# Four planning passes over the main region, ordered first layers of the experts, and scattered expert rows, in a one-core fp32 block kernel

## The chip, the cores and the metric

The kernel runs on one core of one Trainium2 chip. The core has TensorE (PE in the rows: matmuls and transposes; PEld is its weight load), VectorE (DVE), ScalarE (ACT), GpSimd (POOL), SyncE (SP, which here only issues transfers) and 16 DMA engines. The metric is the time of one execution in microseconds of device time. A profiled execution also leaves a trace with the start and end of each instruction, what released it, and the clock granted to TensorE.

## What is computed

512 tokens of width 1024, batch 1, all in fp32. Cut to what matters:

```python
# first block
mod = silu(c) @ ada_w + ada_b                      # 1024 x 3072
shift, scale, gate = split(mod, 3)
h = rmsnorm(x, norm_g) * (1 + scale) + shift
p = h @ w_in
y = concat(rwkv7(p[..., :RWKV_COLS]), stick_breaking(p[..., RWKV_COLS:])) @ w_out
x = rmsnorm(x + gate * y, final_g)
# second block
x = layernorm(a * x + gated_delta_net(x))          # 8 q/k heads, 16 v heads, two directions
for grp in range(4):                               # 32 experts, top 1 of 4 groups, then top 2 of its 8
    h = silu(x @ w_gate[grp]) * (x @ w_up[grp])
    out += (h * comb[grp]) @ w_down[grp]
x = layernorm(a * x + out)
x = x + sigmoid(x @ pe_w_gate) * (p_2 @ pe_w_proj)
```

## The kernel before, in words

**A planner stands behind all code.** `Kern` (phase1, phase2, phase3) never issues an instruction itself. Each call, such as `V.tensor_tensor(...)`, is recorded by `Rec` as an operation with its engine, tiles, cost in a model, and successors. `Rec.run` then lays the tiles out in SBUF and PSUM and emits the operations region by region in the order that `Rec.order` returns. So all instructions have one source line, that of `emit` (L738), and the names of SBUF in the trace are those of memory zones: S_0_87, S_0_90, S_0_94 are arenas that hold many tiles, P_0_135 is PSUM. `order` (L554) is a list scheduler: it walks a model of the five queues forwards, and among the operations of an engine that are ready it takes the one with the highest `rank`, which is the longest chain of costs from the operation to the end (`cp`), plus a bonus per stage (`AHEAD`), plus a little noise. Each engine carries out its own list strictly in that order. `MIX` seeds the random order in which tiles get their places in memory. There are three regions: region 0 is everything up to an If around nine overflow blocks, region 1 is those blocks (skipped with these inputs), region 2 is the end of the kernel. `nc.edge(a, b)` lets the operations b start only after the operations a.

**High and low halves.** A matmul of fp32 values is made of three (`mm3`, L811): each operand is split into a rounded part hi (cast by ACT) and a rest lo (subtraction on DVE, `split`, L794), and hi by hi, hi by lo and lo by hi are added up in PSUM. So each piece of weights costs an ACT cast and a DVE subtraction.

**Setup (phase1, L838).** The four token chunks of x are loaded, scaled and transposed into `xnT` (8 tiles of 128 features by 512 tokens). `mod` has 24 columns of 128: each is a dot product of a 128 x 1024 piece of `ada_w` with c, on DVE (`scalar_tensor_tensor` with `accum_out`). For each of the 8 tiles k two columns (scale 8+k, shift k) are needed before h is formed by a DVE `tensor_scalar` and split into `hTh` and `hTl`, on which the matmuls with `w_in` wait. The columns 16 to 23 are the gate, used only behind `out1`, far later; their loads and dot products stand in the code behind the 8 tiles of h.

**Middle.** RWKV and stick breaking are generators whose steps are interleaved by `STEPS` (L762, L1260), then `out1`, then the gated delta net: heads, `prep`, and for four groups (gq) of heads `invert` (L1508), which inverts 32x32 triangles on DVE in a chain of 60 dependent steps of shrinking width (`inv32`, L1313) between DVE transposes, then `scan` and `finish`. Then layer norm and the routing (L1827 on), where a one-hot matmul `ptab` gives for each of 16 blocks of 112 slots (NP = 16, NS = 112, NB = 25) the token `gidx` that a slot holds.

**Experts (L2039 `block`).** Block b serves two experts, s = 0 and 1. POOL gathers its 112 rows (`xe`, indirect DMA from x_d), PE transposes them (112x112), and for each s: the first layer `pgu` (24 matmuls of 128x512, gate and up at once), silu on ACT, product with the mask on DVE (`hs`), two transposes of `hs`, a split into `hT`; then the second layer `pd` (12 matmuls per s). Weights come by SP into a ring of 22 pieces `raw` of 512 KB, 12 pieces per block. The result `ys` is copied by ACT and written by SP to rows b*112 and on of `y_d`. Blocks 16 to 24 of `y_d` are filled with zeros by SP, with 9 writes from the middle of the kernel.

**End (L2110 on).** POOL gathers for each chunk of 128 tokens and each of its two experts the rows of `y_d` by `yidx` (8 indirect DMAs of 128 x 1024), DVE adds them with their weights, then layer norm, transposes, the matmuls of the output gate, and the result.

## Time and profile before

| | |
|---|---|
| three runs | 1583.02, 1584.03 (median), 1599.12 us |
| the profiled execution | 1593.17 us; its span (first to last instruction) 1591.3 us |
| PE busy | 1436.6 us (90%), PEld 1189.3 us (75%) |
| DVE, ACT, POOL busy | 1151.9 us (72%), 963.3 us (61%), 193.8 us (12%) |
| transfers | 273.40 MB, mean 172 GB/s |
| mean granted TensorE clock | 0.953 |

Busy times say how long an engine was at work, not whether it was waited for. Since PE is busy for 90% of the span, what matters is where the other 10% lies and what ended each of its waits. So the table by stage comes first, and then the waits inside a stage.

### The profile page before, as it was taken

What the parts mean: (1) busy time and instruction counts of PE and PEld (TensorE: products, weight loads), DVE (VectorE), ACT (ScalarE), POOL (GpSimd) and SP (SyncE); (2) the same over time, 40 slices, a digit from 0 to 9 for tenths busy, and PEclk for the clock granted to TensorE, in tenths of its full rate; (3) what the DMA queues carried; (4) which work ended last, traced back from release to release, by engine and by line L of the source; (5) the groups of instructions that cost most, each with busy time, mean ns of one, the idle gap of its engine ahead of it and who ended that gap; (6) DMA issues with size and microseconds to landing.
All of it is one profiled execution on the core that took longest, in us unless ns stands there. A gap on an engine that the chain in (4) does not pass through costs nothing. (4 is left out here: it accounts for less than half of the span.)

```text
span 1591.3 us, 25168 instructions
## 1 busy us (share of the span) xinstructions
PE 1436.6 (90%) x8865; PEld 1189.3 (75%) x8865; DVE 1151.9 (72%) x2281; ACT 963.3 (61%) x2029; POOL 193.8 (12%) x334
## 2 busy tenths in 40 slices
PE   5989999999989885999999999999958999999948
PEld 3677777777978764887988788988847777777736
DVE  7995348865565589898995797553567888888863
ACT  4426455555246876579677856663447777777821
POOL 2101111112010222012101300000120000000040
PEclk7999999799999897999999999999969999999969
DMA  9321111214333754234523641575268999999442
GB/s 379 120 80 54 41 49 58 97 41 132 107 119 113 220 192 146 69 118 156 164 99 129 199 136 58 195 283 209 91 224 276 348 361 355 346 362 354 149 163 80
DMA packets 118023, 273.40 MB, mean 172 GB/s; under 512 B 12416, under 2 KB 53632, under 8 KB 116864
## 3 DMA queue, kind: packets, MB, share of 16 engines
q1 hardware_dynamic: 114688, 263.31, 47.5%
q0 software_dynamic: 3200, 8.39, 1.6%
q8 instruction: 72, 1.18, 0.3%
q14 instruction: 63, 0.52, 0.1%
HBM read 231.81 MB, written 42.99 MB: 173 GB/s over the span
## 5 line engine op out<-in xcount | busy, mean ns | idle before, releaser
L738 PE MATMUL P<-S 128*128 128x512 f32 (+6 forms) x4659 | 942.7, 340 | 91.2 <-DVE S L738 50.6
L738 PEld LDWEIGHTS P<-S 128*128 128x128 f32 (+3 forms) x4659 | 676.5, 181 | 231.2 <-DVE S L738 65.6
L738 PE MATMUL P<-S,S 128*128 128x512 f32 (+12 forms) x4206 | 765.7, 315 | 57.1 <-DVE S L738 43.0
L738 PEld LDWEIGHTS P<-S,S 128*128 128x128 f32 (+4 forms) x4206 | 560.1, 178 | 163.9 <-DVE S L738 35.1
L738 DVE TENSOR_TENSOR S<-S,S 128x512 fp32r<-128x512 f32 (+17 forms) x607 | 474.4, 804 | 171.4 <-ACT S L738 136.2
L738 ACT CAST S<-S 128x512 fp32r<-128x512 f32 (+2 forms) x457 | 365.7, 821 | 293.8 <-PE P L738 238.5
L738 ACT ACTIVATE S<-S 128x128 f32<-128x128 f32 (+7 forms) x433 | 209.2, 517 | 89.8 <-DVE S L738 59.6
L738 DVE SCALAR_TENSOR_TENSOR S<-S 128x512 f32<-128x512 f32 (+3 forms) x302 | 182.6, 632 | 46.2 <-ACT S L738 36.1
L738 DVE TENSOR_TENSOR S<-S 128x256 f32<-128x256 f32 (+32 forms) x414 | 148.5, 372 | 9.2 <-ACT S L738 3.0
L738 ACT COPY S<-P 128x512 f32<-128x512 f32 (+5 forms) x224 | 109.1, 497 | 70.7 <-PE P L738 65.0
L738 ACT ACTIVATE S<-P,S 128x128 f32<-128x128 f32 (+1 forms) x325 | 110.5, 411 | 58.3 <-PE P L738 48.7
L738 ACT ACTIVATE S<-P 128x512 f32<-128x512 f32 (+6 forms) x226 | 87.0, 401 | 54.0 <-PE P L738 49.7
L738 POOL TENSOR_SCALAR_AFFINE_SELECT S<-S 128x128 f32<-128x128 f32 (+2 forms) x137 | 62.0, 466 | 325.7 <-DVE S L738 118.0
L738 DVE TENSOR_TENSOR S<-P,S 128x512 f32<-128x512 f32 (+4 forms) x131 | 75.2, 586 | 31.8 <-ACT S L738 26.1
L738 POOL MEMSET S<- 128x2 f32 (+9 forms) x102 | 27.0, 275 | 365.8 <-DVE S L738 353.4
L738 DVE SCALAR_TENSOR_TENSOR S<-P,S,S 128x128 f32<-128x128 f32 (+2 forms) x165 | 58.4, 366 | 15.7 <-PE P L738 14.3
L738 DVE SCALAR_TENSOR_TENSOR S<-S,S 128x128 f32<-128x128 f32 (+5 forms) x121 | 54.8, 485 | 12.3 <-POOL S L738 7.8
L738 DVE SCALAR_TENSOR_TENSOR S<-S,P 128x128 f32<-128x128 f32 (+2 forms) x112 | 45.0, 429 | 24.7 <-PE P L738 20.1
L738 POOL TENSOR_TENSOR S<-S,S 128x8 f32<-128x8 f32 (+2 forms) x22 | 35.2, 1601 | 219.3 <-DVE S L738 218.5
L738 ACT CAST S<-P 128x224 fp32r<-128x224 f32 (+2 forms) x80 | 36.0, 477 | 39.4 <-PE P L738 38.2
L732 ACT ACT_TABLE_LOAD x45 | 57.7, 1283 | 0.8
L738 POOL DMA_INDIRECT S<-x_d,S x16 | 25.4, 1588 | 255.7 <-PE P L738 237.9
(34 smaller groups left out, 318.7 us busy)
## 6 DMA issues: line engine op xcount, KB each, us to landing
S<-in_moe_w_dram SPq DMA_DIRECT2D x192, 512.0 KB, 6.9
S<-in_gw_in_dram SPq DMA_DIRECT2D x48, 512.0 KB, 4.4
S<-in_w_in_dram SPq DMA_DIRECT2D x29, 512.0 KB, 3.5
S<-in_ada_dram SPq DMA_DIRECT2D x24, 512.0 KB, 8.5
y_d<-S SPq DMA_DIRECT2D x25, 448.0 KB, 6.5
gdn<-S SPq DMA_DIRECT2D x40, 256.0 KB, 3.1
S<-gdn SPq DMA_DIRECT2D x8, 1280.0 KB
S<-gcT_d SPq DMA_DIRECT2D x64, 128.0 KB, 3.3
```

The costliest lines, as they stand in the source:

```text
L732: self.nc.scalar.preload_act_table_set(o.load)
L738: return getattr(self.real[o.eng], o.method)(*[real(x) for x in o.args], **{n: real(x) for n, x in o.kw.items()})
```

## The change

Six edits, in one diff:

1. `Rec.plan` schedules region 0 up to four times (`PASSES`). After each pass `back` walks the finished schedule backwards with the same model of the queues and writes into `tail` how long before the end each operation has to start; the next pass ranks by `tail` in place of `cp`. The pass whose model ends earliest is kept. `MIX` goes from 18 to 13, which places tiles elsewhere.
2. The eight gate columns with their loads move into a group "mod" behind the fourth of the interleaved RWKV and stick-breaking steps.
3. h is formed by ACT (`activation`, Identity, with scale and bias columns) in place of a DVE `tensor_scalar`.
4. `y_d` has one row per token and expert choice (2 x 512 rows). A block writes its rows with an indirect DMA on POOL to the rows in `sidx` (slots without a token are dropped), the end reads 8 plain pieces by SP, and the zero writes are gone. For this `ptab` has 76 columns in place of 50.
5. `gu_last`: the first matmul of each first layer `pgu` waits for the last matmul of the first layer before it, over s and over blocks.
6. `yidx` is gone, `sidx` is computed by one more DVE operation and two ACT operations.

```diff
-    MIX = 18
+    MIX = 13
+    PASSES = 4
+    def back(self, ids):
...
+                    heapq.heappush(q, (-ops[i].start - 1e9 * ops[i].held, i))
...
+            o.tail = end
...
+    def plan(self, ids, t0):
...
+        for k in range(self.PASSES):
...
+            got = self.order(ids, t0, k)
+            end = max(ops[i].end for i in ids)
+            if best is None or end < best[0]:
...
-            o.rank = o.cp + self.AHEAD.get(o.group, 0.0) + 1e9 * o.held
+            o.rank = (o.tail if k else o.cp) + self.AHEAD.get(o.group, 0.0) + 1e9 * o.held
...
-                    for i in self.order(ids, self.t_end):
+                    for i in (self.order if n else self.plan)(ids, self.t_end):
...
-            V.tensor_scalar(xnT[:, k], xnT[:, k], mod[:, 8 + k:9 + k], mod[:, k:k + 1], ALU.mult, ALU.add)
+            A.activation(xnT[:, k], xnT[:, k], AF.Identity, scale=mod[:, 8 + k:9 + k], bias=mod[:, k:k + 1])
...
-        for j in range(16, 24):
-            aw = pp.tile([P, D], F32, name="awg", bufs=2)
-            nc.sync.dma_start(aw, I["ada"][j])
-            V.scalar_tensor_tensor(aw, aw, 0.5, cbc, ALU.mult, ALU.mult, accum_out=mod[:, j:j + 1])
+        def gate_columns(after):
+            gp = nc.pool("ag")
+            for j in range(16, 24):
+                aw = gp.tile([P, D], F32, name="awg", bufs=2)
+                nc.edge(after, [nc.sync.dma_start(aw, I["ada"][j])])
...
+            if n == 3:
+                nc.group("mod")
+                gate_columns([nc.ops[-1]])
...
-        y_d = nc.dram([NB * NS, D], F32, name="y_d")
-        zero = cp.tile([NS, P], F32, name="zero")
-        G.memset(zero, 0.0)
-        for b in range(NP, NB):
-            nc.sync.dma_start(y_d[b * NS:(b + 1) * NS].rearrange("s (x d) -> s x d", d=P),
-                              zero[:, None, :].to_broadcast([NS, D // P, P]))
+        y_d = nc.dram([2 * SEQ, D], F32, name="y_d")
...
-        ohi = lp.tile([P, 8, 2, NB], F32R, name="ohi")
+        ohi = lp.tile([P, 8, 3 * NB + 1], F32R, name="ohi")
...
+        V.scalar_tensor_tensor(sidx, ptab[0:NS, 0:NB], -1.0, pf, ALU.add, ALU.add)
...
+                        gu += self.mm3(pgu, xT[0][:, kk], xT[1][:, kk], wh[:, sl], wl[:, sl], kk == 0, kk == KD - 1)
+
+                nc.edge(self.gu_last, gu[-24:-23])
+                self.gu_last = gu[-1:]
...
-            nc.sync.dma_start(y_d[b * NS:(b + 1) * NS], ys.rearrange("p a b -> p (a b)"))
+            G.indirect_dma_start(out=y_d, out_offset=At(sidx[:, b:b + 1]), in_=ys.rearrange("p a b -> p (a b)"),
+                                 in_offset=None, bounds_check=2 * SEQ - 1, oob_is_err=False)
...
-                G.indirect_dma_start(out=yy, out_offset=None, in_=y_d, in_offset=At(yidx[:, k, c:c + 1]),
-                                     bounds_check=NB * NS - 1, oob_is_err=False)
+                nc.sync.dma_start(yy, y_d[k * SEQ + c * P:k * SEQ + (c + 1) * P])
```

**Where the order changes.** The rows below are the instructions of one engine in the order in which it carries them out; x2 at the end of a row means two in a row.

DVE in the setup, near the last tile of h. A SCALAR_TENSOR_TENSOR of 128x1024 is one column of `mod`, a TENSOR_SCALAR of 128x512 is one tile of h, a TENSOR_TENSOR of 128x512 is a lo part (of h or of a weight). Before:

```order
L738 SCALAR_TENSOR_TENSOR S_0_90<-S_0_90,S_0_87 128x1024 x2
L738 TENSOR_TENSOR S_0_90<-S_0_90,S_0_87 128x1
L738 SCALAR_TENSOR_TENSOR S_0_87,S_0_90<-S_0_87 128x1024
L738 TENSOR_SCALAR S_0_90<-S_0_90 128x512
L738 TENSOR_TENSOR S_0_94<-S_0_87,S_0_198 128x512
L738 TENSOR_TENSOR S_0_94<-S_0_90,S_0_94 128x512
L738 SCALAR_TENSOR_TENSOR S_0_90<-S_0_90,S_0_87 128x1024
L738 SCALAR_TENSOR_TENSOR S_0_87,S_0_90<-S_0_87 128x1024
```

Now:

```order
L831 SCALAR_TENSOR_TENSOR S_0_87<-S_0_87 128x1024 x2
L831 TENSOR_TENSOR S_0_87<-S_0_87 128x1 x2
L831 SCALAR_TENSOR_TENSOR S_0_87<-S_0_87 128x1
L831 TENSOR_TENSOR S_0_199<-S_0_96,S_0_199 128x512
L831 TENSOR_TENSOR S_0_94<-S_0_87,S_0_94 128x512
L831 TENSOR_TENSOR S_0_199<-S_0_96,S_0_199 128x512
L831 TENSOR_TENSOR S_0_199<-S_0_87,S_0_94 128x512
```

Five of the eight gate columns stood ahead of the last lo part of h on DVE; none of them does now, and the rows of 128x512 that formed h are gone from this engine.

DVE at the end of the first 32x32 inverse of the gated delta net. A TENSOR_TENSOR of 128xAxB with A + B = 31 is a step of the inverse; SCALAR_TENSOR_TENSOR of 128x128 is a step of `prep`, of 128x512 a step of the convolution of a later head; TENSOR_TENSOR of 128x512 is a lo part; TENSOR_SCALAR and RECIPROCAL of 128x4 belong to a head's norms. Before:

```order
L738 TENSOR_TENSOR S_0_390<-S_0_390,S_0_87 128x4x27
L738 SCALAR_TENSOR_TENSOR S_0_90<-S_0_87 128x128
L738 TENSOR_TENSOR S_0_87<-S_0_390 128x3x28
L738 SCALAR_TENSOR_TENSOR S_0_90<-S_0_87 128x128
L738 TENSOR_TENSOR S_0_390<-S_0_390,S_0_87 128x3x28
L738 SCALAR_TENSOR_TENSOR S_0_90<-S_0_87 128x128
L738 TENSOR_TENSOR S_0_87<-S_0_390 128x2x29
L738 SCALAR_TENSOR_TENSOR S_0_90<-S_0_87 128x128
L738 TENSOR_TENSOR S_0_390<-S_0_390,S_0_87 128x2x29
L738 SCALAR_TENSOR_TENSOR S_0_90<-S_0_87 128x128
```

Now:

```order
L831 TENSOR_TENSOR S_0_96<-S_0_96,S_0_87 128x4x27
L831 SCALAR_TENSOR_TENSOR S_0_87<-S_0_87 128x512
L831 TENSOR_TENSOR S_0_87<-S_0_87,S_0_96 128x3x28
L831 SCALAR_TENSOR_TENSOR S_0_87<-S_0_87 128x512
L831 TENSOR_TENSOR S_0_96<-S_0_96,S_0_87 128x3x28
L831 TENSOR_SCALAR S_0_87<-S_0_87 128x4
L831 TENSOR_TENSOR S_0_199<-S_0_96,S_0_199 128x512
L831 TENSOR_TENSOR S_0_87<-S_0_87,S_0_96 128x2x29
L831 SCALAR_TENSOR_TENSOR S_0_87<-S_0_87 128x512
L831 TENSOR_TENSOR S_0_96<-S_0_96,S_0_87 128x2x29
L831 RECIPROCAL S_0_87<-S_0_87 128x4
L831 SCALAR_TENSOR_TENSOR S_0_87<-S_0_87 128x512
```

From the two transposes ahead of the inverse to those behind it, 32 rows of 128x128, 18 SCALAR_TENSOR_TENSORs of 128x512 and 11 lo parts stood among its 60 steps; now it is 1 row of 128x128, 20 and 16.

PE in the expert stage, at the change from one block to the next. A row of 128x112 is transposes (four of the next block's rows, or two of `hs`), the rows of 128x512 are first and second layers. Before:

```order
L738 MATMUL P_0_135<-S_8899_9165,S_0_94 128x512 x2
L738 MATMUL P_0_135<-S_0_94 128x512 x6
L738 MATMUL P_0_135<-S_0_87 128x112 x6
L738 MATMUL P_0_135<-S_8899_9165,S_0_94 128x512 x2
L738 MATMUL P_0_135<-S_0_94 128x512 x2
L738 MATMUL P_0_135<-S_8899_9165,S_0_94 128x512 x4
L738 MATMUL P_0_135<-S_0_87 128x112
L738 MATMUL P_0_135<-S_0_94 128x512 x2
```

Now:

```order
L831 MATMUL P_0_135<-S_0_199,S_8889_9178 128x512 x30
L831 MATMUL P_0_135<-S_0_87 128x112 x2
L831 MATMUL P_0_135<-S_0_199,S_8889_9178 128x512 x9
L831 MATMUL P_0_135<-S_0_87 128x112 x4
L831 MATMUL P_0_135<-S_0_199,S_8889_9178 128x512 x2
L831 MATMUL P_0_135<-S_0_199 128x512 x2
L831 MATMUL P_0_135<-S_0_199,S_8889_9178 128x512 x2
L831 MATMUL P_0_135<-S_0_199 128x512
L831 MATMUL P_0_135<-S_0_199,S_8889_9178 128x512 x2
L831 MATMUL P_0_135<-S_0_199 128x512
L831 MATMUL P_0_135<-S_0_87 128x112 x2
L831 MATMUL P_0_135<-S_0_199 128x512 x2
```

Before, both first layers of a block end together, and four transposes of the next block and the first two of `hs` follow at once (x6), then second-layer matmuls that need that `hs`. Now the transposes of `hs` of s = 0 (the first row x2) come with seventeen of the 24 first-layer matmuls of s = 1 ahead of them, and those of s = 1 (the second row x2) with twelve matmuls between them and the end of that first layer, two of them of the next block. In the last block the last transposes of `hs` have eleven second-layer matmuls ahead of them and one behind them that doesn't need them.

## Rows read from the trace of the kernel before

**Rows 1.** Busy time by stretch: us, busy us (instructions) per engine, clock, DMA share, GB/s.
```profile
20.00:35.00 15.00, 9.31 (x17) 4.92 (x18) 15.00 (x41) 3.95 (x7) 0.00 (x0) 0.50 1.03 409
35.00:60.00 25.00, 22.34 (x88) 15.81 (x86) 23.07 (x48) 8.95 (x16) 0.80 (x2) 0.95 0.61 226
60.00:520.00 460.00, 442.51 (x3226) 362.27 (x3226) 300.89 (x599) 237.75 (x437) 58.20 (x112) 0.97 0.24 81
520.00:640.00 120.00, 90.80 (x498) 75.31 (x497) 96.42 (x222) 89.61 (x207) 29.05 (x62) 0.86 0.57 183
640.00:1160.00 520.00, 504.64 (x3404) 441.94 (x3402) 381.38 (x933) 339.36 (x976) 56.01 (x98) 0.99 0.43 148
1160.00:1240.00 80.00, 58.31 (x240) 45.65 (x240) 54.35 (x116) 46.05 (x66) 12.45 (x6) 0.81 0.78 260
1240.00:1480.00 240.00, 222.88 (x1018) 175.34 (x1017) 201.51 (x218) 180.79 (x241) 12.96 (x10) 1.00 0.97 349
...
1513.00:1535.00 22.00, 0.25 (x1) 0.25 (x2) 13.63 (x16) 3.71 (x6) 11.27 (x10) 0.55 0.69 241
1535.00:1591.30 56.30, 49.79 (x224) 39.77 (x223) 27.05 (x45) 12.67 (x22) 4.98 (x6) 0.92 0.23 75
```

**Rows 2.** Costliest groups by form, DVE, 0 to 60 us: busy us, mean ns.
```profile
L738 DVE SCALAR_TENSOR_TENSOR S<-S 128x1024 f32<-128x1024 f32 x14 | 16.9, 1222 | 7.6 <-ACT S L738 6.5 <-DMA S<-in_ada_dram 1.1
...
L738 DVE TENSOR_SCALAR S<-S 128x512 f32<-128x512 f32 x8 | 4.7, 593 | 0.0
```

**Rows 3.** The same, ACT, 0 to 130 us: an ACTIVATE with operand columns.
```profile
L738 ACT ACTIVATE S<-S,S 128x512 f32<-128x512 f32 x2 | 1.4, 724 | 0.3 <-DVE S L738 0.3
```

**Rows 4.** Timeline of PE around the first inverse: start, us, instructions [idle before].
```profile
600.85 4.38 PE L738 MATMUL P<-S 128*128 128x128 f32 x22 [0.78 <-DMA S<-gdn]
621.41 0.98 PE L738 MATMUL P<-S,S 128*128 128x128 f32 x3 [16.18 <-DVE S L738]
```

**Rows 5.** Groups by form, DVE, 569 to 616 us (the inverse).
```profile
L738 DVE SCALAR_TENSOR_TENSOR S<-S 128x512 f32<-128x512 f32 x18 | 13.6, 754 | 0.1
L738 DVE SCALAR_TENSOR_TENSOR S<-S 128x128 f32<-128x128 f32 x32 | 11.2, 349 | 0.3 <-ACT S L738 0.3
L738 DVE TENSOR_TENSOR S<-S,S 128x512 fp32r<-128x512 f32 x10 | 7.1, 705 | 0.6 <-ACT S L738 0.6
```

**Rows 6.** Timeline of PE at the change of an expert block.
```profile
1346.74 0.41 PE L738 MATMUL P<-S 112*128 112x112 f32 x2 [0.81 <-DVE S L738]
1347.77 0.73 PE L738 MATMUL P<-S,S 128*128 128x512 f32 x2 [0.61 <-ACT S L738]
```

**Rows 7.** Waits, 1203 to 1513 us, of PE and of SP's queue: us, times, longest.
```profile
PE P L738 <- DVE S L738: 15.9, 16, 3.3
PE P L738 <- ACT S L738: 8.8, 15, 0.6
```
```profile
SPq L738 <- DVE S L738: 225.0, 163, 7.5
```

**Rows 8.** DMA issues of the whole run: count, KB each, median us to landing.
```profile
S<-in_moe_w_dram SPq DMA_DIRECT2D x192, 512.0 KB, 6.9
...
y_d<-S SPq DMA_DIRECT2D x25, 448.0 KB, 6.5
...
S<-x_d,S POOLq DMA_INDIRECT x16, 8.9
```

**Rows 9.** Groups by form, POOL, 1203 to 1513 us.
```profile
L738 POOL DMA_INDIRECT S<-x_d,S x12 | 15.6, 1304 | 231.1 <-PE P L738 231.1
```

**Rows 10.** Timeline after the last block, then of PE alone.
```profile
1513.20 0.33 SPq L738 DMA_DIRECT2D y_d<-S  x1
...
1517.65 1.23 DVE L738 TENSOR_TENSOR S<-S,S 128x1024 fp32r<-128x1024 f32 x1 [0.67 <-ACT S L738]
1519.18 1.02 POOL L738 DMA_INDIRECT S<-y_d,S  x1 [80.70 <-DVE S L738]
```
```profile
1534.75 0.47 PE L738 MATMUL P<-S 128*128 128x128 f32 x1 [22.46 <-DVE S L738]
```

**Rows 11.** Costliest groups of the page: ACT's table loads.
```profile
L732 ACT ACT_TABLE_LOAD x45 | 57.7, 1283 | 0.8
```

More of the change, by code (lines that the diff above doesn't have):

```diff
@@ L234 @@
     __slots__ = ("i", "eng", "method", "args", "kw", "succ", "npred", "ready", "cost", "cp", "vts", "lat", "dma",
-                 "func", "start", "end", "load", "rows", "part", "group", "rank", "array", "held", "port")
+                 "func", "start", "end", "load", "rows", "part", "group", "rank", "array", "held", "port", "tail")
 SETS = {"Exp": ("exp_and_others", "natural_log_exp_and_others"), "Tanh": ("exp_and_others", "silu_and_others"),
@@ L556, in order @@
+    def order(self, ids, t0, k=0):
         ops = self.ops
@@ L1259, in phase1 @@
         sb_v()
-        for step in self.STEPS.split():
+        for n, step in enumerate(self.STEPS.split()):
             nc.group(step)
             next((R if step[0] == "r" else S)[int(step[1])], None)
+            if n == 3:
+                nc.group("mod")
+                gate_columns([nc.ops[-1]])
         nc.group("out1")
@@ L1833, in phase3 @@
         gidx = rp.tile([NS, NB], I32, name="gidx")
-        yidx = rp.tile([P, 2, NCH], I32, name="yidx")
+        sidx = rp.tile([NS, NB], I32, name="sidx")
         oidx = rp.tile([P, NX, 6], I32, name="oidx")
@@ L2119, in phase3 @@
             for b in range(NX):
+                self.gu_last = []
                 block(NP + b, extra_weights(b))
```

96 lines of the change are left out of this document (88 added, 8 removed).

## The prediction

> **What bounds the kernel now.** I read the busy shares first (PE 90%, DVE 72%, ACT 61%), then a table by stretches, then inside each stretch the waits of PE. PE is at work nearly all the time from 60 to 520 us and from 640 to 1160 us (442.51 of 460 and 504.64 of 520 us, granted clock 0.97 and 0.99 of 2.4 GHz) [rows 1]; there nothing but less matmul work could give much, and the change takes no matmul away. What can be gained lies in five places where PE stands still: the setup, the stretch 520 to 640 (29.2 us idle), routing and the start of the experts from 1160 to 1240 (21.7), the experts (17.1 idle in 240 us), and the end from 1513 to 1535 (21.8) [rows 1].
>
> The profiled execution has 1593.17 us, 9.1 above the median 1584.03. I make the sum against the profiled one and take it off the median.
>
> **Setup.** From 20 to 35 us DVE is busy for 15.00 of 15 us, ACT for 3.95, and PE for 9.31 us at clock 0.50, the lower level of 1.2 GHz; the transfers move 409 GB/s [rows 1]. So DVE and the loads together set when each tile of h comes. The change takes from DVE, ahead of the last tile of h, eight instructions of 593 ns and five of the gate columns of 1222 ns [rows 2]: 8 x 0.593 + 5 x 1.222 = 4.7 + 6.1 = 10.8 us. From the loads it takes five pieces of 512 KB, at 409 GB/s 5 x 1.28 = 6.4 us. How much of it PE can use is bounded by what PE loses there: between 20 and 60 us it is idle for 5.7 + 2.7 = 8.4 us, and half of the 9.31 us at the half clock, 4.7, could go too; 13.1 at most. The lower end is the 2.7 us of idle from 35 to 60, if the clock and the first tiles stay as they are. I take **-8**, the idle time and near the loads' 6.4.
>
> ACT gets the eight instructions. The nearest row is an ACTIVATE with operand columns, 724 ns [rows 3], 5.8 us in all, and ACT is idle for 11 of the 15 us. The Trainium skill ("ScalarE: Activation LUTs", Rules for kernel authors) says to use VectorE and not ScalarE for multiply and add. The trace agrees on the single instruction (724 against 593 ns) and not on the stage, since DVE is the full engine there; by the rule alone this edit would give 8 x (724 - 593) = 1.0 us back instead of taking 4.7.
>
> The gate columns return between 60 and 520 us, 8 x 1.222 = 9.8 us on DVE and 4.2 MB of loads; DVE is busy there for 300.89 of 460 us and the DMA share is 0.24 [rows 1], so they cost nothing; without that cover 9.8. Eight columns have up to `out1` to be ready.
>
> **New order in the middle.** The one long wait is 16.18 us on DVE [rows 4]: PE waits for the first inverse, whose 60 dependent steps share DVE's queue with other work. In the new order 31 rows of 349 ns are gone from between the steps, two of 754 and five of 705 ns have come [rows 5]: 31 x 0.349 - 2 x 0.754 - 5 x 0.705 = 10.8 - 1.5 - 3.5 = 5.8 us less. I take **-6**. What is late next is that moved work, the preparation of later heads, but PE has the scan by then. Its bounds are 0, if PE only waits for something else, and -16, the whole wait. For the rest of 60 to 1240 us the new order and memory places can give or cost, and no row says which: idle in all besides that wait is 17.5 + 13.0 + 15.4 + 21.7 = 67.6 us [rows 1]. I take 0, with -14 (a fifth of it) and +10 (DVE and ACT queues stand in a worse order in one or two places) as ends. The order has 49 ACT table loads for 45; four of 1.283 us [rows 11] are 5.1 us on an engine with room, taken as 0, inside the +10. The longer routing matmul and three small operations are below 1 us; the zero writes that go lie at a DMA share of 0.43 or less or before the routing's end, 0.
>
> **Experts.** A block of the steady stretch ends with the same pair of waits, 0.81 us for the product on DVE ahead of the 112x112 transposes and 0.61 us for the split behind them [rows 6]; over the stage PE waits 15.9 us on DVE and 8.8 on ACT, in 31 waits [rows 7]. 16 x 1.42 = 22.7. The transposes now have seventeen or twelve matmuls between them and the layer that they need; at 222.88 us for 1018 [rows 1] that is 12 x 0.22 = 2.6 us at least, more than 1.42. In the last block one matmul (0.22) covers the 0.61, so 0.4 stays. I take **-18**, four fifths of 22.7, since blocks closer together leave DVE, busy for 84% now, at some 90%, and a queue so full adds waits. Ends: 0 and -24.7.
>
> The block's write moves from SP to POOL: 16 scatters; a gather there is 1304 ns [rows 9], so 21 us on an engine that waits for 231. Each stands ahead of the gather of the block four or five later, so it has more than 60 us; a transfer of POOL lands after 8.9 us against 6.5 by SP [rows 8]. Nothing, and -24.7 stays the end.
>
> **End.** PE is idle for 22.46 us until 1534.75 [rows 10]. POOL's eight gathers begin at 1519.18, behind the last split of DVE (1517.65 + 1.23). Eight plain loads of SP begin at about the same time and are bound by their 4.2 MB, 10.3 us at 409 GB/s; eight additions on DVE follow them closely. I take **-2**. Against it stands the last scatter: by the 8.9 us it lands at 1513.2 + 8.9 = 1522.1, 3 us behind the branch, so the ends are -5 and +4.
>
> **Sum.** -8 - 6 + 0 - 18 - 2 = -34 us: 1593.2 to 1559, or off the median 1584.0 - 34 = **1550 us**.
>
> **Rivals.**
> *The weights become the bound.* In the steady stretch the DMA share is 0.97 at 349 GB/s [rows 1] and a piece needs 6.9 us to land [rows 8]. If these are the most that come, 7.0 MB per block (12 pieces, a gather, half a scatter) need 20.1 us and blocks can't come closer than now once the ring is used up. Against it: SP waits 225 us for free slots, that is for DVE to be done with a piece [rows 7], so the ring of 22 is full, and 22 pieces are almost two blocks ahead; PE would take 1.1 us per block off that lead. It would cost at most the half of the gain, **1559**. The Trainium skill ("DMA: Bandwidth & Descriptors", Specifications) gives a limit of about 358 GB/s of HBM per core; by it the steady stretch is at the limit. The trace disagrees at 409 GB/s in the setup.
> *The new order gives more.* With `tail` in place of `cp` in every stage: a further 14 us off the 67.6, **1536**.
> *The new order gives nothing.* The inverse's relief is taken by another wait, the setup gives its 2.7, and the +10 falls due: -2.7 - 18 + 10 - 2 = -13, **1571**, within 1%.
> *Slower.* One mechanism: the sequences that the model now ranks by its own finish are wrong for the delta net, and each of its four groups gets a wait like the one of 16.18 us. Three more of them are +48.5, and with -34 + 6 the sum is +20, **1604**. It decides from the second such wait on, where -28 + 32 passes zero. For it: PE waited so once already. Against it: from 640 to 1160 us, where three of the four groups lie, PE is idle for 15.4 of 520 us [rows 1], so the other inverses are covered by work that is still there.
>
> **Chances.** The sum within some 10 us: 0.52. More from the order: 0.18. Weights as the bound or half of the experts' gain: 0.13. Nothing from the order: 0.11. Slower: 0.06. A measurement of this kernel can tell about 1% from no change, 16 us, so faster is below 1568: the first three and a little of the fourth, less what the third leaves above it: 0.84. Same 0.11, slower 0.05. The range runs from the rival with more (1536, and 8 further for a setup and an inverse at their ends) to the edge of the fourth: 1528 to 1568.
>
> **What would show it.** Setup: the last 128x512 matmul with h comes 8 us earlier, the stretch from 20 us on has less idle and less half clock. Inverse: the one long wait of PE on DVE near 600 us is about 10 us, not 16. Experts: no pair of 0.8 and 0.6 us at each block, a block of under 19 us for 19.85, and no wait of PE on a load. POOL: each scatter issued without a wait of a block. End: idle of PE near 20 us. It is wrong if PE in the experts waits on `in_moe_w` or if new waits on DVE or ACT of several us stand between 640 and 1160 us.

## The result, and the profile after

The changed kernel needs 1542.83 us (median of four runs, 1539.44 to 1546.54) for 1584.43 before: the ratio is 0.9731 [0.9668, 0.9793], 41.6 us less. Medians and ratios here and below leave out executions more than 1.5% above the fastest of their kernel. The two profiled executions differ by 46.6 us, 1593.17 to 1546.54. The forecast was 1550 us, so total and side held; the parts of which the total was made did not. First the page of the kernel after: its span, its busy shares and two groups.

```profile
span 1544.8 us, 25192 instructions
PE 1439.1 (93%) x8865; PEld 1200.3 (78%) x8865; DVE 1148.2 (74%) x2274; ACT 977.7 (63%) x2043; POOL 206.8 (13%) x341
...
L825 ACT ACT_TABLE_LOAD x49 | 62.9, 1283 | 0.9
...
S<-in_moe_w_dram SPq DMA_DIRECT2D x192, 512.0 KB, 8.8
```

Next the table by stretches of the kernel after, with the columns of [rows 1]. The stretches are the same in microseconds, not in work: from the middle on the kernel after is ahead of the one before.

```profile
20.00:35.00 15.00, 11.28 (x31) 7.26 (x32) 14.51 (x39) 9.01 (x15) 0.00 (x0) 1.00 1.02 393
35.00:60.00 25.00, 24.33 (x121) 18.55 (x121) 21.36 (x44) 15.71 (x26) 1.65 (x1) 1.00 0.25 87
60.00:520.00 460.00, 448.05 (x3141) 361.28 (x3137) 302.16 (x607) 236.75 (x442) 57.28 (x114) 0.92 0.25 82
520.00:640.00 120.00, 106.22 (x698) 91.39 (x697) 107.67 (x233) 89.75 (x217) 28.02 (x56) 0.94 0.51 168
640.00:1160.00 520.00, 496.57 (x3262) 436.19 (x3260) 374.27 (x936) 341.17 (x960) 56.50 (x100) 0.98 0.45 154
1160.00:1240.00 80.00, 69.12 (x305) 56.03 (x306) 64.31 (x108) 58.77 (x83) 14.60 (x10) 0.89 0.90 319
1240.00:1440.00 200.00, 198.90 (x939) 162.21 (x939) 185.26 (x203) 171.22 (x224) 29.05 (x20) 1.00 1.00 374
...
1467.00:1489.00 22.00, 0.43 (x3) 0.16 (x2) 16.88 (x19) 7.62 (x10) 3.56 (x3) 0.61 0.75 257
```

Three things are to be seen against [rows 1]. PE in the steady stretch of the experts is busy for 198.90 of 200 us. The idle time from 520 to 640 us is 13.8 instead of 29.2. And from 60 to 520 us PE is *busier* (448.05 for 442.51 us) yet does *fewer* instructions (3141 for 3226), and the granted clock has fallen from 0.97 to 0.92. That is a loss the forecast does not have.

To split the difference by stages I laid the recorded order of each engine beside its rows of the trace, and took the end of the last DVE or ACT instruction of a stage (us from the span's start; one profiled execution each):

| stage ends at | before | after | duration before | duration after | difference |
|---|---|---|---|---|---|
| last lo part of h | 54.4 | 44.0 | 54.4 | 44.0 | -10.4 |
| `out1` | 460.0 | 464.5 | 405.6 | 420.5 | +14.9 |
| layer norm ahead of the routing | 1161.1 | 1155.3 | 701.1 | 690.8 | -10.3 |
| routing | 1193.6 | 1181.1 | 32.5 | 25.8 | -6.7 |
| experts | 1513.2 | 1469.6 | 319.6 | 288.5 | -31.1 |
| end | 1587.7 | 1541.7 | 74.5 | 72.1 | -2.4 |

The sum is -46.0 us. So the experts gave far more than forecast, the setup's gain was lost again ahead of `out1`, and the middle and the routing gave more.

**Experts.** The waits of PE inside the stage (1180 to 1466 us; us, times, longest) answer [rows 7]: there were 15.9 us in 16 and 8.8 us in 15 waits, and all that is left is

```profile
PE P L831 <- ACT S L831: 2.2, 3, 1.1
```

The timeline of PE at the change of a block answers [rows 6]; no row has idle time in brackets any more:

```profile
1339.84 0.35 PE L831 MATMUL P<-S 112*128 112x112 f32 x2
1339.96 0.94 PE L831 MATMUL P<-S,S 128*128 128x512 f32 x3
```

**Inverse.** The waits of PE from 520 to 660 us answer [rows 4], where one wait on DVE alone was 16.18 us; the longest on DVE there is now 1.6:

```profile
PE P L831 <- ACT S L831: 11.3, 10, 2.4
PE P L831 <- DVE S L831: 2.3, 3, 1.6
```

DVE's chain of the inverse stands between two pairs of transposes. The first two rows are before, the next two after; the last is the row of PE that needs the result:

```profile
562.69 4.10 DVE L738 STREAM_TRANSPOSE S<-S 128x1024 f32<-128x1024 f32 x2 [3.55 <-ACT S L738]
...
616.36 3.70 DVE L738 STREAM_TRANSPOSE S<-S 128x1024 f32<-128x1024 f32 x2
```
```profile
539.65 3.92 DVE L831 STREAM_TRANSPOSE S<-S 128x1024 f32<-128x1024 f32 x2 [3.64 <-ACT S L831]
...
587.66 3.92 DVE L831 STREAM_TRANSPOSE S<-S 128x1024 f32<-128x1024 f32 x2
```
```profile
592.50 1.13 PE L831 MATMUL P<-S,S 128*128 128x128 f32 x8 [1.56 <-DVE S L831]
```

From pair to pair it is 53.7 us before and 48.0 after. But it also begins 75.2 us behind `out1` where it was 102.7.

**End.** The last scatter, the eight plain loads, the first sum and the first matmul behind them, on four queues, answer [rows 10]:

```profile
1469.84 1.50 POOL L831 DMA_INDIRECT y_d<-S  x1 [14.61 <-ACT S L831]
...
1475.26 4.71 SPq L831 DMA_DIRECT2D S<-y_d  x8
...
1478.83 1.29 DVE L831 SCALAR_TENSOR_TENSOR S<-S 128x1024 f32<-128x1024 f32 x1 [3.67 <-DMA S<-y_d]
...
1488.84 1.54 PE L831 MATMUL P<-S 128*128 128x128 f32 x6 [21.57 <-DVE S L831]
```

PE waited 22.46 us and waits 21.57.

### The profile page after: what moved, and what is told of

It is laid out like the page before. It is cut to its first block, busy times and chain, and to the rows that moved or that the text cites. A ratio compares the mean times of both kernels' runs of the same rounds, so it can differ in the third digit from the quotient of the medians.

```text
span 1544.8 us, 25192 instructions
## 1 busy us (share of the span) xinstructions
PE 1439.1 (93%) x8865; PEld 1200.3 (78%) x8865; DVE 1148.2 (74%) x2274; ACT 977.7 (63%) x2043; POOL 206.8 (13%) x341
## 5 line engine op out<-in xcount | busy, mean ns | idle before, releaser
L831 PE MATMUL P<-S 128*128 128x512 f32 (+8 forms) x4513 | 848.1, 330 | 56.9 <-DVE S L831 24.7
L831 PE MATMUL P<-S,S 128*128 128x512 f32 (+8 forms) x4352 | 841.6, 330 | 42.8 <-DVE S L831 30.8
L831 PEld LDWEIGHTS P<-S 128*128 128x128 f32 (+5 forms) x4513 | 639.3, 183 | 172.1 <-ACT S L831 35.1
L831 PEld LDWEIGHTS P<-S,S 128*128 128x128 f32 (+4 forms) x4352 | 605.7, 180 | 165.9 <-DVE S L831 42.3
L831 DVE TENSOR_TENSOR S<-S,S 128x512 fp32r<-128x512 f32 (+13 forms) x715 | 500.9, 724 | 110.6 <-ACT S L831 91.0
L831 ACT ACTIVATE S<-S 128x128 f32<-128x128 f32 (+4 forms) x514 | 235.6, 498 | 93.3 <-DVE S L831 66.6
L831 DVE SCALAR_TENSOR_TENSOR S<-S 128x512 f32<-128x512 f32 (+4 forms) x336 | 198.9, 627 | 46.6 <-ACT S L831 31.8
L831 DVE TENSOR_TENSOR S<-S 128x256 f32<-128x256 f32 (+18 forms) x306 | 119.9, 401 | 10.3 <-ACT S L831 4.1
L831 DVE TENSOR_TENSOR S<-P,S 128x512 f32<-128x512 f32 (+3 forms) x131 | 75.1, 586 | 35.5 <-ACT S L831 21.3
L831 POOL TENSOR_TENSOR S<-S 128x8 f32<-128x8 f32 (+3 forms) x34 | 51.1, 1502 | 198.8 <-DVE S L831 197.5
```

What stands on the lines that cost most here:

```text
L831: return getattr(self.real[o.eng], o.method)(*[real(x) for x in o.args], **{n: real(x) for n, x in o.kw.items()})
```

## The experiments

Each kernel is planned anew, except the last three of the table, which start from the order of after. So an edit can also change the order elsewhere, and I read each by its stages. The table has what the text below uses: the ratio to the kernel before on the same chip (medians 1584.43 to 1588.23 us) with its interval, then, from one profiled execution, the end of the last lo part of h and of `out1`, the granted clock from 130 to 230 us, and the durations from `out1` to the layer norm, of the experts and of the end (us).

| kernel | median us | ratio | last lo | `out1` | clock | to norm | experts | end |
|---|---|---|---|---|---|---|---|---|
| before | 1584.43 | 1 | 54.4 | 460.0 | 1.00 | 701.1 | 319.6 | 74.5 |
| after | 1542.83 | 0.9731 [0.9668, 0.9793] | 44.0 | 464.5 | 0.71 | 690.8 | 288.5 | 72.1 |
| before, with the edges of `gu_last` | 1556.73 | 0.9815 [0.9779, 0.9851] | 54.3 | 459.6 | 1.00 | 702.8 | 287.3 | 75.5 |
| after, without them | 1552.49 | 0.9796 [0.9732, 0.986] | 45.9 | 459.3 | 0.86 | 690.8 | 293.2 | 74.1 |
| after, gate columns in the setup | 1553.08 | 0.98 [0.9773, 0.9828] | 55.5 | 460.0 | 0.97 | 704.9 | 285.7 | 76.4 |
| after, h on DVE | 1568.4 | 0.9841 [0.9767, 0.9914] | 46.0 | 477.6 | 0.76 | 697.3 | 286.1 | 72.9 |
| after, one pass | 1599.23 | 1.0053 [1.001, 1.0095] | 43.9 | 490.9 | 0.74 | 729.6 | 290.8 | 73.2 |
| after, `MIX` 18 | 1565.32 | 0.9823 [0.9773, 0.9872] | 43.0 | 478.7 | 0.78 | 694.2 | 280.1 | 73.7 |
| after, no scatter | 1582.16 | 0.9966 [0.9936, 0.9996] | 44.2 | 487.4 | 0.74 | 703.3 | 288.4 | 75.4 |
| after, gate at step 1 | 1555.2 | 0.9777 [0.972, 0.9834] | 42.5 | 485.0 | 0.74 | 688.7 | 285.2 | 73.8 |
| after, gate at step 5 | 1551.7 | 0.9761 [0.9679, 0.9843] | 44.1 | 463.6 | 0.78 | 703.2 | 286.6 | 74.3 |
| after, dots moved in its order | 1534.17 | 0.9657 [0.9628, 0.9685] | 45.3 | 454.2 | 0.98 | 692.6 | 288.0 | 73.8 |
| after again, same chip as the row above | 1550.23 | 0.9749 [0.9714, 0.9784] | 44.1 | 458.6 | 0.85 | 690.1 | 289.1 | 72.3 |
| after, dots in gaps | 1530.62 | 0.9653 [0.9602, 0.9705] | 45.5 | 443.2 | 0.97 | 693.7 | 288.5 | 72.1 |

The kernel after stands in it twice: the second time, on another chip, its median is 7.4 us higher. A difference of that size between medians from different chips says nothing about an edit.

### Where the gain of the experts comes from

The kernel before, with edit 5 alone:

```diff
+                        gu += self.mm3(pgu, xT[0][:, kk], xT[1][:, kk], wh[:, sl], wl[:, sl], kk == 0, kk == KD - 1)
...
+                nc.edge(self.gu_last, gu[-24:-23])
+                self.gu_last = gu[-1:]
```

> The kernel before with the ordered first layers alone (the edges of gu_last, one planning pass, nothing else of the change). Theory A: the pair of waits at each expert block, with what PE loses in draining and refilling around them, goes by the edges alone, and they carry the gain of the expert stage: it lasts 323.4 us from the first 112x112 transposes to the last matmul in the kernel before and 289.9 in the changed one, so here 290 to 298, and the whole about 1553 to 1562 us. Rival B: the ranking by the backward pass orders the experts, the edges matter little: the stage stays at 315 or more, the whole at 1575 or more. Order outside the experts may move by some us.

The stage took 287.3 us, 32.3 less (from the first transposes to the last matmul 291.1, inside the expected 290 to 298), and the median is 27.9 below that of the kernel before on the same chip, 1584.67. Waits of PE over the stage, then its steady stretch in the columns of [rows 1]:

```profile
PE P L738 <- DVE S L738: 0.7, 2, 0.4
```
```profile
1220.00:1450.00 230.00, 229.74 (x1083) 184.52 (x1082) 209.15 (x231) 191.69 (x257) 12.43 (x11) 1.00 1.01 383
```

PE stands still for 0.26 us in 230. The edges alone do the whole work in the experts, and leave all other stages within 1.7 us of before. The transfers give 383 GB/s where the kernel before had 349.

The kernel after, without the edge:

```diff
-                nc.edge(self.gu_last, gu[-24:-23])
```

> The changed kernel without the edges of gu_last, so that the four passes rank the first layers alone. Theory A: the two first layers of a block end together again, the waits of 0.8 and 0.6 us come back at each block, the expert stage has 310 to 325 us instead of 289.9 and the whole is 1562 to 1578. Rival B: the backward pass keeps them apart by itself, the stage stays within 6 us of 289.9 and the whole at 1537 to 1550.

The stage took 293.2 us, 4.7 more than after and 26.4 less than before. Its waits of PE:

```profile
PE P L831 <- DVE S L831: 2.9, 4, 1.4
PE P L831 <- ACT S L831: 2.1, 3, 1.1
```

So the new order, with the planner's own rank, separates the first layers nearly as well; whether by the passes or by the places of the tiles this run doesn't tell. Either way is enough for most of it, and the two don't add up. I had put the gain down to the edges alone; in the new order they are worth 4.7 us of the stage.

### What the two edits of the setup bring

The kernel after with the gate columns back behind the eight tiles of h:

```diff
-            gp = nc.pool("ag")
+            gp = pp
...
-                nc.edge(after, [nc.sync.dma_start(aw, I["ada"][j])])
+                nc.sync.dma_start(aw, I["ada"][j])
...
+        gate_columns([])
...
-            if n == 3:
...
-                nc.group("mod")
-                gate_columns([nc.ops[-1]])
```

> The changed kernel with the gate columns back in the setup, h still by ScalarE. The setup should lose what the gate columns take ahead of the last tile of h: up to five dot products of 1.22 us, so the last lo part of h at 48 to 51 us instead of 44. Theory C: no gate column is left among the 64-wide state steps, so no half-clock stretch there, and the whole comes out faster than the changed kernel all the same, 1520 to 1532. Rival D: the half clock stays and the whole is 1546 to 1556.

The last lo part ends at 55.5 us, 1.1 later than before, though h is on ACT, and later than the expected 48 to 51. The half clock is all but gone (0.97), as expected of theory C, but the total of 1553.08 us is far from its 1520 to 1532: the norm comes 704.9 us behind `out1`. The first row below is the setup: the transfers are back at 409 GB/s, and PE is busy for 9.35 us, near the 9.31 of [rows 1]. The second row has its clock further on:

```profile
20.00:35.00 15.00, 9.35 (x23) 6.58 (x23) 14.17 (x36) 7.54 (x12) 0.00 (x0) 0.81 1.03 409
...
130.00:230.00 100.00, 99.47 (x816) 75.01 (x815) 41.26 (x94) 59.98 (x107) 14.34 (x33) 0.97 0.13 43
```

The kernel after with h on DVE again:

```diff
-            A.activation(xnT[:, k], xnT[:, k], AF.Identity, scale=mod[:, 8 + k:9 + k], bias=mod[:, k:k + 1])
+            V.tensor_scalar(xnT[:, k], xnT[:, k], mod[:, 8 + k:9 + k], mod[:, k:k + 1], ALU.mult, ALU.add)
```

> The changed kernel with h formed by VectorE as before (eight instructions of 593 ns back on DVE, off ScalarE); the gate columns stay moved. By the prediction's sum the last lo part of h comes 4.7 us later than in the changed kernel, 48.7 instead of 44.0 us. Rival, from the run with the gate columns in the setup, where h on ScalarE alone left the last lo part at 55.5 us against 54.4 before: the engine of h is worth nothing, the gate columns and their loads are the whole gain of the setup, and the last lo part stays at 43 to 46 us; the whole within 8 us of 1543 unless the half-clock stretch changes.

The last lo part ends at 46.0: 8.4 us of the 10.4 come without h on ACT, with the gate columns and their loads moved. For h at most 2.0 are left, where 4.7 stood in the sum, and they are not resolved: the other kernels that have h on ACT and the gate columns moved end this part at 42.5 to 45.9 us. With the gate columns still in the setup, h on ACT gives nothing (1.1 later). So what held the setup were the gate's loads and columns; that the forming of h holds it once these are gone is not shown. The total is 25.6 us above the first median of after (18.2 above the second), but 13.1 us of it lie ahead of `out1` and 6.5 between `out1` and the norm, in orders that the planner changed; that is no price of the edit.

### What passes, places and scatters are worth

```diff
-    PASSES = 4
+    PASSES = 1
```

> The changed kernel with one planning pass in place of four: all other edits stay. If the four passes are what shortened the way from the end of the RWKV part to the end of routing (in the changed kernel 716.6 us from the last DVE instruction of out1 to the last of the routing, before 733.6), it goes back to 728 to 736 here; the expert stage stays at 286 to 292 us since the edges alone gave 287.3. Whole: 1545 to 1562, and less if the half clock at 172 to 229 us, which the kernel before did not have, belongs to the new order of the passes: then the part up to the end of out1 is near 449 instead of 464.5 and the whole near 1540. Rival: the gain of the middle comes from the other edits (places in memory, routing table), and it stays at 714 to 720.

With one pass all other edits together are no gain (1545 to 1562 was expected). The experts still take 290.8, so the edges do their work, but `out1` comes at 490.9 and the stretch to the norm takes 729.6 instead of 690.8. The profiled execution is the longest of ten, 1620.04 us, so these two are at the upper end. But the long wait at the first inverse is back, and the chain begins 103.8 us behind `out1`, near the 102.7 of before:

```profile
653.27 2.05 PE L831 MATMUL P<-S,S 128*128 128x128 f32 x8 [12.48 <-DVE S L831]
```

So it is in all profiles: in the eleven with four passes the chain begins 75 to 85 us behind `out1` and PE waits there for DVE 3.5 us at most; in the three with one pass (before, before with the edges, and this one) it is 102 to 104 us and 12.5 to 16.5. The passes took this wait away.

```diff
-    MIX = 13
+    MIX = 18
```

> The changed kernel with the number before, 18 in place of 13, for the places of the tiles in memory; the four passes then plan another order. The three runs that planned anew (one pass, h on VectorE, no scatter) lay 20 to 60 us above the changed kernel, nearly all of it ahead of the experts, in half-clock stretches and waits. If the planner's order is that chancy, this one is also above: 1550 to 1590, with the expert stage within 285 to 291 us all the same. Rival: the three were slower for their own edits, and a mere change of places stays within 10 us of 1543.

A different placing of the tiles, and the order that the planner makes for it, costs about 22 us (15 against the second median of after), most of it ahead of `out1` (478.7). The 280.1 us of its experts are short only because the last instruction of its routing is late: from the first transposes to the last matmul it takes 288.5 us, after 289.9. So with the old places all the other edits give 0.9823, no more than the edges alone with 0.9815; what the kernel after has beyond that came only together with the places of number 13. How much of the loss with one pass, beyond the wait at the inverse, is such chance isn't resolved either.

The last of this group undoes edit 4, but for the wider routing table:

```diff
...
-            G.indirect_dma_start(out=y_d, out_offset=At(sidx[:, b:b + 1]), in_=ys.rearrange("p a b -> p (a b)"),
-                                 in_offset=None, bounds_check=2 * SEQ - 1, oob_is_err=False)
+            nc.sync.dma_start(y_d[b * NS:(b + 1) * NS], ys.rearrange("p a b -> p (a b)"))
...
-                nc.sync.dma_start(yy, y_d[k * SEQ + c * P:k * SEQ + (c + 1) * P])
+                G.indirect_dma_start(out=yy, out_offset=None, in_=y_d, in_offset=At(yidx[:, k, c:c + 1]),
+                                     bounds_check=NB * NS - 1, oob_is_err=False)
```

> The changed kernel with the plain writes of the expert rows by SP, the zero writes and the gathers of the end by POOL as before (nothing of edit 4 but the wider routing table). The scatter was forecast as free in the experts and worth 2 us at the end: expert stage 287 to 292 us, end 72.5 to 75.5 us instead of 72.1 from the last ACT copy of the experts, whole 1541 to 1550 if the half clock stays as it is. Rival: with blocks closer together the zero writes and larger writes cost transfer time, and the expert stage is 295 us or more.

The experts take 288.4 us with SP's writes and 288.5 with POOL's scatters: the scatters are free. The end takes 75.4 for 72.1, but the end of the same code varies from 72.1 to 76.4 over the kernels above, so the few microseconds of the plain loads are not resolved. The median is 39 us longer than the first of after (32 than the second, and 1541 to 1550 us were expected); in the profiled execution that lies ahead of the experts (`out1` at 487.4, 703.3 to the norm), in an order planned anew.

### Where the setup's gain went

In the kernel after, the first RWKV state steps (matmuls of 64x64 and 128x64) run at the half clock. The first row is the stage of these steps before, from their start; the second is the stretch after in which the clock is low. They don't hold equal work (404 and 332 matmuls):

```profile
168.00:209.00 41.00, 40.21 (x404) 28.44 (x403) 15.70 (x52) 19.45 (x50) 5.08 (x10) 1.00 0.05 15
```
```profile
172.00:229.00 57.00, 57.00 (x332) 39.32 (x329) 18.15 (x48) 22.12 (x43) 5.61 (x14) 0.50 0.03 10
```

At 0.50, the level of 1.2 GHz, PE is busy for all of 57 us. What it did before the fall is seen in the next rows, of DVE and then of PE. DVE's queue has a gate column's dot product, which waits for its load of `ada_w`; the small operations of the state chain stand behind it; PE then waits for DVE:

```profile
169.98 1.23 DVE L831 SCALAR_TENSOR_TENSOR S<-S 128x1024 f32<-128x1024 f32 x1 [1.76 <-DMA S<-in_ada_dram]
```
```profile
171.63 0.48 PE L831 MATMUL P<-S,S 128*64 128x64 f32 x4 [1.82 <-DVE S L831]
```

I summed (1 - granted clock) x busy time of PE in slices of 5 us from 60 us to `out1`: 11.9 us before, 35.0 after. That is 23.1 us more; with the 5.5 us less of idle time from 60 to 520 us (17.5 to 11.95) it leaves 17.6, near the 14.9 us of the stage table.

The Trainium skill ("TensorE: Matmul & The Clock Gate", A second HAM failure mode) tells of a kernel in which short pauses between groups of matmuls were enough to move the clock between its two levels. The trace agrees in that only a short wait stands at the fall, here one of 1.82 us among small matmuls; it differs in that the clock then stayed low while PE was busy. That the wait is the cause no run shows.

Two runs put the columns at other steps of the interleaving:

```diff
-            if n == 3:
+            if n == 1:
```

> The changed kernel with the gate columns behind the second of the interleaved steps instead of the fourth: their eight dot products then stand on DVE ahead of the first head group's chain of 64-wide state steps, not among it. In the changed kernel a dot product waits 1.76 us for its load there, PE then stands 1.82 us, and the granted clock is at the lower level from 172 to 229 us while PE is busy all the time. Theory C: that wait lowers the clock; without it the stretch runs at 2.4 GHz and the kernel takes 20 to 28 us less, 1515 to 1525. Rival D: the stretch of small matmuls (64x64 and 128x64) lowers the clock whatever DVE does there: a half-clock stretch of 40 us or more stays, and the time is within 6 us of 1543.

```diff
-            if n == 3:
+            if n == 5:
```

> The changed kernel with the gate columns behind the sixth of the interleaved steps instead of the fourth. Theory E, after the run with the columns behind the second step: the stretch of 64-wide matmuls of the first RWKV half has only some 40 matmuls of 512 columns in it in every order and falls to the lower clock when PE stands still for over about a microsecond in it (1.8 us in the changed kernel, 1.3 behind the second step; 0.8 and 0.5 without a fall). If PE idles less than 0.8 us there now, the stretch runs at full clock and the whole is 1515 to 1530; with idle of 1.3 us or more it falls, 1538 to 1550. Rival: it falls without any such idle, or doesn't in spite of it.

The half clock stayed in both. At step 1 the last dot ends at 161.9 us, 16 us before the fall, and yet the clock fell, at a wait of PE on ACT, seen in PE's timeline and in the table for the stage:

```profile
178.06 0.88 PE L831 MATMUL P<-S,S 64*64 64x64 f32 x6 [1.34 <-ACT S L831]
```
```profile
160.00:220.00 60.00, 58.37 (x421) 41.59 (x421) 18.75 (x57) 22.71 (x55) 4.88 (x13) 0.65 0.06 18
```

With the columns at step 5 only one wait of 0.61 us stood among the state steps ahead of the fall, which speaks against theory E. So a dot product that waits is not needed for the fall. Nor do the waits of PE among the state steps, added up, tell the kernels apart cleanly: where the clock held they were 0.79 us (before), 0.46 (gate in the setup), 0.76 and 0.77 (the two kernels with moved dots, below); where the clock fell they were 0.97 to 1.82 ahead of the fall, but for these 0.61.

To leave the rest of the order as it is, the two kernels with moved dots plan as after does, take the group "mod" out of the finished list, and put it back at other places in DVE's list; all other operations of region 0 keep the order of after:

```diff
+    START, STEP = 206, 2
...
+    def gate_later(self, got):
...
+        mod = [i for i in got if ops[i].group == "mod"]
+        rest = [i for i in got if ops[i].group != "mod"]
...
-                    for i in (self.order if n else self.plan)(ids, self.t_end):
+                    got = (self.order if n else self.plan)(ids, self.t_end)
+                    for i in got if n else self.gate_later(got):
```

> The changed kernel with its own planned order on every engine, in which only the gate group (8 loads, 8 dot products, 1 addition) is put about 20 DVE instructions earlier, so that none stands among the 64-wide state steps of the first RWKV half; nothing is planned anew, so nothing else moves. Theory C: the dot product that waits for its load (1.76 us) stops PE for 1.82 us and this alone drops the clock; without it no half clock from 172 to 229 us, and the whole is 20 to 28 us below the changed kernel, 1515 to 1523. Rival D: the fall comes with a setup that ends 11 us earlier, whatever DVE does there (it came in every order with the gate columns out of the setup, in none with them in it): a half-clock stretch of 25 us or more stays, 1535 to 1548.

> The changed kernel once more, on the same chip as the run with the moved dot products, for a comparison run by run: 1538 to 1552 us, a ratio to the kernel before of 0.970 to 0.978, with the half-clock stretch from 172 to about 229 us.

The two ran on the same chip. The moved dots give 1534.17 for 1550.23 us, 16 us, and the intervals of their ratios lie apart; against the first four executions of after, 1542.83 us, it is 8.7, and there the intervals overlap a little. The two profiled executions are close, 1538.27 and 1540.42 us, but the one is the longest of its five and the other the second shortest of its six. The mean clock over the span is 0.959 to 0.971 with the moved dots and 0.948 to 0.961 without. In the stage the clock is full, and `out1` comes at 454.2, 10.3 us earlier than in the first profile of after and 4.4 earlier than in the second:

```profile
160.00:204.00 44.00, 43.11 (x413) 29.53 (x413) 17.06 (x53) 21.12 (x52) 4.72 (x10) 1.00 0.05 16
```

It is less than I had expected, 1515 to 1523 us. The dots now stand in an earlier chain of the RWKV on DVE, and PE waits for it there:

```profile
136.54 4.31 PE L850 MATMUL P<-S,S 128*128 128x512 f32 x18 [2.32 <-DVE S L850]
```

The state steps so begin at 160.6 us, 6.6 later than in after. The repeated kernel of after shows how unsteady the clock is: with the same instructions in the same order the stretch 172 to 229 us has a clock of 0.73 here where it had 0.50, since the low clock begins at 172.4 us and ends near 203, after 31 us. PE's longest wait ahead of it is 0.68 us, not 1.82 (first row):

```profile
169.26 0.92 PE L831 MATMUL P<-S,S 64*128 64x256 f32 x4 [0.68 <-DVE S L831]
```
```profile
172.00:229.00 57.00, 56.84 (x376) 41.15 (x377) 22.20 (x52) 25.84 (x48) 10.47 (x17) 0.73 0.06 19
```

Its `out1` comes at 458.6 instead of 464.5, and its profiled execution takes 1540.42 instead of 1546.54 us: 5.9 and 6.1 us.

The last run spreads the dots over gaps of DVE, by a list of places instead of a step (the rest as in the first of the two, but for the loads):

```diff
+    DOTS = (210, 210, 218, 218, 221, 224, 227, 227, 227)
...
+        at = {vec[190]: loads[:2]}
+        for k, i in enumerate(dots):
+            at.setdefault(vec[self.DOTS[k]], []).extend([i] + loads[k + 2:k + 3])
```

> The changed kernel's own order once more with only the gate group moved: now behind the first 32x32 inverse and ahead of the state steps, in the places where the changed kernel's DVE stands still for 4.4, 5.6, 1.9 and 3.2 us waiting for ScalarE. With the dots placed about 20 instructions earlier the half clock of the state steps was gone, but they stood in the inverse, PE waited 2.32 us at 136 us and the first state step came at 160.6 instead of 154.0 us. Theory C: here the first state step comes at 154 to 157 us, no half-clock stretch of over 10 us stands between 150 and 230, and the whole is 3 to 10 us below that run, 1524 to 1531. Rival D: the earlier state steps meet a thinner stretch of matmuls, PE idles in it and the clock falls again: 1535 or more.

The profiled execution took 1528.72 us; `out1` comes at 443.2, 21.3 us earlier than in after, and the first state steps begin at 155.35. The stage has the full clock:

```profile
154.00:200.00 46.00, 45.10 (x423) 30.57 (x423) 17.18 (x53) 21.36 (x54) 4.74 (x10) 1.00 0.12 35
```

Its six runs reach from 1525.66 to 1553.06 us, with mean clocks over the span from 0.970 down to 0.951 and, by and large, the longer times at the lower clocks. In some executions the clock falls, as it seems, all the same; no trace shows one of them. Both kernels with moved dots beat before, and by their medians after; the first is the steadier (1533.02 to 1538.27).

## Why the prediction was right or wrong

That the total came out within 7 us is in part luck. Between the profiled executions the experts gave 13.1 us more than forecast, the routing 6.7, the middle 4.3 and the setup 2.4, and 14.9 us that the sum has nowhere were lost ahead of `out1`.

**Experts, -18 forecast, -31.1 measured.** The mechanism was right: the pair of waits at each block is gone, and no PE wait on a load has come. The size failed at "four fifths of 22.7". There was no reason to leave a fifth: DVE, whose fuller queue was to add waits, is busy for 93% (185.26 of 200 us) and adds nearly none. And the sum left out a term. The first two rows below are the stage from the first transposes to the last matmul, before and after. Idle time fell by 22.6 us (24.7 to 2.2), and PE's *busy* time fell by 11.1 (298.86 to 287.73) with the same 1344 instructions:

```profile
1188.70:1512.30 323.60, 298.86 (x1344) 235.06 (x1344) 266.76 (x307) 243.57 (x324) 16.63 (x13) 0.99 0.89 316
```
```profile
1177.36:1467.27 289.91, 287.73 (x1344) 233.90 (x1344) 261.90 (x291) 242.74 (x319) 38.53 (x28) 0.99 0.92 342
```
```profile
1240.00:1440.00 200.00, 185.73 (x848) 146.13 (x847) 167.89 (x182) 150.72 (x201) 12.96 (x10) 1.00 0.98 353
```

In the steady stretch (last row, before), at the same clock of 1.00, a matmul takes 185.73 / 848 = 219.0 ns before and 198.90 / 939 = 211.8 after; over 84 matmuls and transposes in each of 16 blocks that is 9.7 us. I read it as what PE loses beside each wait. Counted from start to start, without the wait itself, in the trace of before, the row ahead of a wait took 259 ns where rows of its kind elsewhere in the stage took 31 or 108, and the first row behind a wait 152 or 338 ns where others took 108 or 240. Over the 31 waits that is some 8 us. The other 3 lie in undisturbed rows, 240 against 235 ns for 128x512, and why is open.

**The weights as the bound: refuted.** A piece lands after 8.8 us instead of 6.9, but the transfers move 374 GB/s in the steady stretch (383 with the edges alone) and PE waits for none. So the 349 of before was not a limit. The Trainium skill ("DMA: Bandwidth & Descriptors", Bandwidth) gives its 358 GB/s for two cores that stream at once, and 425 for one; the trace of this single core agrees that 358 is no limit for it, with 374 to 409 GB/s.

**Setup, -8 forecast; -10.4 at the last lo part, +4.5 at `out1`.** DVE's relief was put at 10.8 us and the loads' at 6.4; 10.4 came, but 8.4 of it by the loads and the columns; h on ACT gave 2.0 at most, not resolved, and nothing as long as the columns stood there. The Trainium skill ("ScalarE: Activation LUTs", Rules for kernel authors) prefers VectorE for such an operation; whether h on ACT costs the 1.0 us that the prediction worked out from this rule or gains a little, the runs don't decide, and the 4.7 did not come.

The step that failed is the sentence that the gate columns "cost nothing" since DVE is busy for 300.89 of 460 us. A busy share says that the work fits; it doesn't say where in the queue it stands. Each queue is carried out in order, and a dot product that waits for its load holds the small steps of a dependent chain behind it. PE's own stop was only 1.82 us, but 57 us at 1.2 GHz followed. Moving nothing but the gate's loads and dots in an otherwise equal order took 16 us off the median on the same chip; this is the part that is shown. That this wait alone makes the clock fall is not: with the dots elsewhere it also fell, and with equal instructions in the same order it fell at waits of 0.68 us and less.

**Middle, -6 forecast, -10.3 measured from `out1` to the norm.** The sum of removed and added rows was right for what it counted: the chain of the first inverse is 5.7 us shorter, for the 5.8 of the sum. But the long wait went nearly as a whole, 16.18 to 1.56, because the chain begins 27.5 us earlier behind `out1` and PE has other matmuls while it runs; the sum had looked at DVE's queue inside the chain and not at where the chain stands. With one pass the chain begins as late as before and the wait is back with 12.48 us. The waits on ACT from 520 to 660 us stayed, 11.3 us in 10 for 11.6 in 4. From 640 us to the norm PE waits 19.5 us for 14.9 before, so part of the gain is given back there.

**"The rest of the middle 0": lucky.** It was a sum of unlike things: with one pass and the same edits the norm comes 65.2 us later (490.9 + 729.6 for 464.5 + 690.8, in a long execution), with another number for the places 17.6 us later. The rival that gives nothing (1571) and the slower one (1604) were thus nearer than their chances of 0.11 and 0.06 said: small edits gave 1551 to 1582 us, and one pass 1599.23. Nothing in the profile of before could tell which order the planner would hit.

**Routing, 0 forecast, -6.7 measured.** The wait of PE for the first gather is 8.98 us where it was 13.86. I had not looked at it; no run was spent on its cause.

**End, -2 forecast, -2.4 measured,** and not resolved, since kernels with the same end differ by 4.3 us. PE's idle time there is 21.57, not "near 20".

**What would show it.** Held: earlier h, a wait of well under 10 us at the inverse, no pair at a block, a block of 288.5 / 16 = 18.0 us, no wait on a load. Failed: the scatters do wait, 119.1 us in 14 waits on ACT over the stage, but for their own `ys`, and nobody waits for them; less half clock in the setup was bought with more of it behind; and one of the two signs of being wrong came: between 640 and 1160 us there are new waits of PE on ACT of 4.88 and 3.18 us, and one on DVE of 3.75 in the routing, where 1.89 was the longest before. They add up to a few microseconds and did not turn the result.

```profile
PE P L831 <- ACT S L831: 14.7, 13, 4.9
PE P L831 <- DVE S L831: 8.5, 7, 3.8
```

## What to carry to other kernels

A dependent transpose between two layers costs PE more than its idle time shows: here 24.7 us of waits came with some 8 us more in the rows beside them. Put an independent layer between. Work moved into an engine's spare time has to be judged by its place in that engine's queue: if it waits for a load, everything behind it does. Where a planner makes the order anew for each edit, compare the stages, or replay one order with only the edited instructions moved; the medians of kernels planned anew here lay 9 to 39 us above the first median of after (and 1 to 32 above its second) where little of it could be traced to the edit itself.

## What the runs showed of the hardware

A stage of 64-wide matmuls stayed at 1.2 GHz for 57 us with PE busy for 57.00 of them; it had fallen at a wait of 1.82 us. In the same kernel, with the same order, another execution fell at waits of 0.68 us and less and was back at full clock after 31 us; a wait of 0.61 us went before a fall in one kernel while 0.79 in two waits did not in another. What decides it is open. One core's transfers held 374 to 383 GB/s for 200 us and more.
